# Three calls that make weight pieces further ahead around a Strassen-form down projection (hybrid encoder, one core)

## The chip, the cores and the metric

The kernel runs on one core of a Trainium2 chip. The metric is device time in microseconds (us), the median of several runs. Where a traced execution is used, its own time and span stand beside it.

## The reference

Two residual layers on 512 tokens of width 1024, each a token mixer followed by a gated MLP. Layer 0 mixes by gated linear attention, layer 1 by grouped-query softmax attention. The change touches the MLP alone, which is the same in both layers:

```python
def conv_ffn(h, w_up, w_conv, b_conv, w_down):
    u = h @ w_up
    u = lax.conv_general_dilated(
        u, w_conv[:, None, :], window_strides=(1,), padding=[(1, 1)],
        dimension_numbers=('NWC', 'WIO', 'NWC'), feature_group_count=u.shape[-1]) + b_conv
    val, gate = jnp.split(u, 2, axis=-1)
    return (jax.nn.silu(gate) * val) @ w_down
...
        x = x + conv_ffn(rmsnorm(x, norm_ffn[i]), ffn_w_up[i], ffn_w_conv[i],
                         ffn_b_conv[i], ffn_w_down[i])
```

`w_up` is 1024 x 5632 and `w_down` 2816 x 1024, all in float32.

## The kernel before

**Arithmetic.** Every float32 operand of a matmul is split in a high half (a copy to fp32r, made by ScalarE) and a low half (the rest, made by VectorE, or by a negated copy and an accumulating DMA from POOL's queue, `flush`). Each product is three matmuls, high x high, high x low, low x high (`mm3`).

**The MLP of a layer** (`ffn`, L658). The 22 tiles of 128 hidden features are walked in order, m = 0 to 21. `act_up(m)` (L664) computes two up tiles of 128 x 512 sums, t = 0 for the value into a PSUM bank of tag "acc" (three banks) and t = 1 for the gate into one of tag "s" (two banks), 24 matmuls each. What is called convolution m here follows in the trace: L683 scales the sums by the norm, L685 to L687 form the width-3 convolution, once for each t; then L689 and L690 apply the gate.

**The down projection** has two forms. Tiles 0 to 15 go pairwise into a seven-product (Strassen-like) form in two *parts* of four pairs: part 0 stands at m = 9 and part 1 at m = 17 (`DOWN_AFTER`, L45). `prepare` (L699) builds the sums of activations of a pair. `down_part` (L723) walks four *strips* of weights, n = 0 to 3, with seven products of 12 matmuls of 128 x 256 in each (L741); `begin(n)` (L745) is a strip's first product. For part 0 the pair of tiles 8 and 9 is prepared inside the part, at L777. Tiles 16 to 21 are *plain*: `split` at L796 writes their halves into a tile that L795 takes from the 22 buffers of tag "g", and they are multiplied in a last stage (L806 on).

The matmuls of `begin(0)` are traced between up tiles (m, 0) and (m, 1), at L673; the rest of the part behind convolution m, at L804.

**The weights** (class `Weights`, L111). `todo` is one list of all pieces in a fixed order. Around a part it reads: up(m, 0), strip 0 piece 0, up(m, 1), strip 0 pieces 1, 2, 3, strip 1 pieces 0 to 3, and so on. `piece(src, i, h, ahead)` (L200) flushes, makes pieces from the list until the wanted one is there, then makes more until `ahead` pieces beyond it are made, and returns it. To make a piece of an up strip is a load of 1 MB by SP's queue into one of two raw buffers (for a strip's first piece), L194 on ScalarE and L195 on VectorE. A down strip holds four blocks a21, a11, a12, a22 in one raw buffer and has four pieces, made by `summed` (L144):

- piece 0: two sums on VectorE (L151 into a new "g" tile of L149, L152 in place), then L177 and L178 for the halves
- piece 1: a third sum (L156), halves into `sh` and `sl`, of which there is one buffer each
- piece 2: two copies on ScalarE (L173, L174), the low half finished by a POOL DMA at the next flush (L184)
- piece 3: a fourth sum (L163), halves L165 and L166

The high and low halves of the other pieces have three buffers each.

**The order of work.** The source order is the order of the trace. The framework then orders each engine's queue at build time: among the instructions that its own model of time holds ready, the one that was traced first goes ahead. So an instruction that is traced late may run early, in a gap, and one that is traced early has precedence; TensorE's queue is ordered in the same way. Waits and buffer assignments are made by the framework.

Of the kernel before, what the change touches and what calls it, by code (L numbers as in the profile page):

```python
# [44 lines left out]
DOWN_AFTER = {9: 0, 17: 1}  # L45
# [9 lines left out]
def hybrid_encoder_kernel(  # L55
# [36 lines left out]
    def bank(tag, n):  # L92
        return pp.tile([P, S], F32, tag=tag, bufs=PS[tag], name=nm(n))
# [4 lines left out]
    def big(dt, n):  # L98
        return pair("g", 22, dt, n)

    def tmp(tag, n, w=S):
        return sp.tile([P, w], F32, tag=tag, bufs={"u": 4, "t": 6, "sq": 3}[tag], name=nm(n))
# [110 lines left out]
    W = Weights()  # L213
    up = [w_up[i] for i in range(2)]
# [127 lines left out]
    def feature_steps(wh, wl, hl, ps):  # L342

        for k in range(KC):
            sl = slice(k * P, (k + 1) * P)
            mm3(ps, wh[:, sl], wl[:, sl], *hl[k], k == 0, k == KC - 1)
            if k == 2:
                W.flush()
            yield

    def feature_tile(*a):
        for _ in feature_steps(*a):
            pass
# [303 lines left out]

    def ffn(layer, norm, cw, nxt):  # L658
        w_dn = down_w[layer]
        plain = {}  # L660
        down = []
        quads = {}

        def act_up(m):  # L664

            res, pss = [], []
            for t in range(2):
                ps = bank("s" if t else "acc", "up")
                feature_tile(*W.half(up[layer], 2 * m + t, 3 if m in DOWN_AFTER and t else 1), norm.hl, ps)
                pss.append(ps)  # L670
                if t == 0 and m in DOWN_AFTER:
                    down.append(down_part(DOWN_AFTER[m], m))
                    next(down[-1])  # L673
                if m == 0 and t == 0:
                    norm.tokens()
                elif m == 0:
                    norm.rows()
            for t in range(2):
                ps = pss[t]
                cc = ((layer * 2 + t) * FC + m) * 4  # L680
                w = lambda i: cw[:, cc + i : cc + i + 1]
                u = tmp("u", "u")
                dve.tensor_tensor(u, ps, norm.R, ALU.mult)  # L683
                y = tmp("t", "y")
                act.activation(y, u, AF.Identity, scale=w(1), bias=w(3))  # L685
                dve.scalar_tensor_tensor(y[:, 1:], u[:, : S - 1], w(0), y[:, 1:], ALU.mult, ALU.add)  # L686
                dve.scalar_tensor_tensor(y[:, : S - 1], u[:, 1:], w(2), y[:, : S - 1], ALU.mult, ALU.add)  # L687
                res.append(y)
            act.activation(res[1], res[1], AF.Silu)  # L689
            dve.tensor_tensor(res[0], res[0], res[1], ALU.mult)  # L690
            return res[0]
# [100 lines left out]
        for m in range(FC):  # L792
            y = act_up(m)
            if m >= 2 * NQ * NPART:
                t = big(F32R, "gu")  # L795
                split(y, t)  # L796
                plain[m] = (t[:, :S], t[:, S:])
            elif m % 2 == 0:
                last = y
            elif m not in DOWN_AFTER:  # L800
                prepare(m // 2, last, y)
            if m in DOWN_AFTER:
                late = last, y
                for _ in down[-1]:  # L804
                    pass
# [224 lines left out]
    norms = [Norm(i) for i in range(4)]  # L1030
    cw = gla(norms[0], norms[1])
    ffn(0, norms[1], cw, norms[2])
    attention(norms[2], norms[3])
    ffn(1, norms[3], cw, None)


# [86 lines left out]
```

## Time and profile before

| | us |
|---|---|
| median of three runs | 1139.58 |
| lowest and highest | 1138.07, 1140.77 |
| the profiled execution, device time | 1138.57 |
| the profiled execution, span of its instructions | 1136.4 |
| TensorE matmul busy in the span | 1119.8 |
| VectorE busy in the span | 795.5 |
| ScalarE busy in the span | 551.6 |

How to read the lines that follow in the prediction. PE is TensorE, DVE is VectorE, ACT is ScalarE, POOL is GpSimd; PEld is the load of weights into TensorE, which overlaps its matmuls. A line of the order of time has the start, the duration, the engine, the source line, the operation, output and input; in brackets stands the idle time of the engine just ahead of it and what ended it. A line of the groups has the busy time and the mean in ns of one instruction, then the idle time ahead of the group. Matmuls are pipelined, so that a matmul of 128 x 512 is listed with 0.39 us and the next one starts 0.23 us after it. A line of the table by stretches has the stretch, its length, and for each engine busy time and count. A busy matmul says nothing of its clock: the granted clock stands in a column of its own (1.00 is full).

### The profile page before, as it was taken

The page shows a single profiled execution, that of the slowest core. Times are in us where ns is not written, and L with a number is a line of the kernel's source. Part 1 is how long each engine was busy: PE and PEld are TensorE (multiplying, and loading weights), DVE is VectorE, ACT ScalarE, POOL GpSimd, SP SyncE. Part 2 cuts the span into 40 slices and gives each one's busy share as a digit, 9 for nine tenths or more (in the row PEclk, how much of TensorE's full clock was granted, in tenths as well). Part 3 has the DMA queues.
Part 4 walks back from the last instruction along what each step waited for, and adds up shares of the span by engine and source line. Part 5 has one row for each costly group of instructions (what it writes and reads, how often), then busy time and mean ns, then how long its engine had stood idle before and what let it go on. Part 6 is the DMA issues. An engine that isn't in the chain of part 4 may idle for free.

```text
span 1136.4 us, 14630 instructions
## 1 busy us (share of the span) xinstructions
PE 1119.8 (99%) x5836; PEld 960.1 (84%) x5836; DVE 795.5 (70%) x1220; ACT 551.6 (49%) x818; POOL 120.2 (11%) x114
## 2 busy tenths in 40 slices
PE   9999999999999999899999999999999999989998
PEld 7888888888889888798888888888888998879887
DVE  6787563667889577775765689766788957777572
ACT  5565233435457344463464667644445634446340
POOL 0104110001011001000004433000100100100000
PEclk9999999999999999899999999999999999999999
DMA  6422211222335332353247633223223543235321
GB/s 230 149 74 79 83 62 38 78 108 74 108 97 154 125 111 74 94 152 127 93 126 189 149 75 75 57 75 111 74 87 107 159 130 111 75 93 149 127 77 74
DMA packets 22291, 120.14 MB, mean 106 GB/s; under 512 B 2640, under 2 KB 3280, under 8 KB 10704
## 3 DMA queue, kind: packets, MB, share of 16 engines
q1 hardware_dynamic: 17328, 102.29, 26.4%
q0 software_dynamic: 4608, 16.78, 7.7%
q8 instruction: 45, 0.74, 0.3%
q14 instruction: 22, 0.18, 0.0%
q10 hardware_dynamic: 288, 0.15, 0.0%
HBM read 100.34 MB, written 2.10 MB: 90 GB/s over the span
## 4 chain that ended last, share of the span: by engine, by line
PE 92%; DVE 3%; issue 2%; DMA 1%; ACT 1%; POOL 0%; SPq 0%; DVEq 0%; POOLq 0%; ACTq 0%
PE up L338 13%; PE up L339 13%; PE up L340 13%; PE r L741 12%; PE vg L369 8%; PE op L395 8%; PE dn L339 2%; PE dn L340 2%; PE dn L338 2%; PE o L620 2%; PE pt L984 1%; DMA wl<-raw 1%; PE av L369 1%; PE kv L596 1%; PE A L338 1%
## 5 line engine op out<-in xcount | busy, mean ns | idle before, releaser
L338 PE MATMUL up<-xhl,wh 128*128 128x512 f32 x704 | 275.3, 391 | 0.0
L339 PE MATMUL up<-xhl,wh 128*128 128x512 f32 x704 | 274.7, 390 | 0.0
L340 PE MATMUL up<-xhl,wl 128*128 128x512 f32 x704 | 274.2, 390 | 0.0
L194 ACT ACTIVATE wh<-raw 128x1024 fp32r<-128x1024 f32 x132 | 139.5, 1057 | 228.0 <-PE up L339 108.2
L195 DVE TENSOR_TENSOR wl<-raw,wh 128x1024 fp32r<-128x1024 f32 x132 | 164.6, 1247 | 40.4 <-ACT wh L194 40.4
L340 PEld LDWEIGHTS up<-xhl,wl 128*128 128x128 f32 x704 | 132.4, 188 | 27.6
L338 PEld LDWEIGHTS up<-xhl,wh 128*128 128x128 f32 x704 | 132.5, 188 | 27.2
L339 PEld LDWEIGHTS up<-xhl,wh 128*128 128x128 f32 x704 | 132.6, 188 | 27.0
L741 PE MATMUL r<-gu,wh 128*128 128x256 f32 x640 | 119.6, 287 | 8.3 <-ACT wh L177 8.1
L741 PEld LDWEIGHTS r<-gu,wh 128*128 128x128 f32 x640 | 101.5, 195 | 10.0 <-ACT wh L177 9.6
L683 DVE TENSOR_TENSOR u<-up,R 128x512 f32<-128x512 f32 x88 | 60.3, 687 | 58.6 <-PE up L340 58.6
L741 PE MATMUL r<-gu,wl 128*128 128x256 f32 x320 | 91.5, 287 | 2.6 <-DMA wl<-raw 2.5
L685 ACT ACTIVATE y<-u,cw 128x512 f32<-128x512 f32 x88 | 71.2, 811 | 42.9 <-DVE u L683 42.9
L369 PE MATMUL vg<-wh,xhl 128*128 128x512 f32 x256 | 80.2, 392 | 0.5 <-DVE halfneg L256 0.5
L686 DVE SCALAR_TENSOR_TENSOR y<-u,cw,y 128x511 f32<-128x511 f32 x88 | 65.6, 747 | 8.3 <-ACT y L685 8.3
L395 PE MATMUL op<-oT,wh 128*128 128x512 f32 x256 | 70.9, 395 | 0.0
L687 DVE SCALAR_TENSOR_TENSOR y<-u,cw,y 128x511 f32<-128x511 f32 x88 | 65.8, 750 | 2.3
L689 ACT ACTIVATE y<-y 128x512 f32<-128x512 f32 x44 | 27.8, 633 | 77.6 <-DVE y L687 77.6
L741 PEld LDWEIGHTS r<-gu,wl 128*128 128x128 f32 x320 | 61.9, 194 | 3.8 <-DMA wl<-raw 3.2
L184 POOL DMA_DIRECT2D wl<-raw x32 | 28.3, 885 | 327.3 <-ACT wl L138 157.6
L369 PEld LDWEIGHTS vg<-wh,xhl 128*128 128x128 f32 x256 | 48.5, 190 | 10.7 <-ACT sq L312 0.7
L395 PEld LDWEIGHTS op<-oT,wh 128*128 128x128 f32 x256 | 47.1, 188 | 9.6 <-ACT oT L635 0.3
(220 smaller groups left out, 1990.9 us busy)
## 6 DMA issues: line engine op xcount, KB each, us to landing
raw<-in_w_up_dram SPq DMA_DIRECT2D x44, 1024.0 KB, 4.8
raw<-in_w_down_dram SPq DMA_DIRECT2D x22, 1024.0 KB, 4.8
wl<-raw POOLq DMA_DIRECT2D x32, 512.0 KB, 4.6
raw<-in_w_vg_dram SPq DMA_DIRECT2D x6, 1024.0 KB, 4.8
raw<-in_w_akq_dram SPq DMA_DIRECT2D x5, 1024.0 KB, 5.0
raw<-in_w_kq_dram SPq DMA_DIRECT2D x4, 1024.0 KB, 4.8
raw<-in_w_gout_dram SPq DMA_DIRECT2D x4, 1024.0 KB, 4.7
raw<-in_w_aout_dram SPq DMA_DIRECT2D x4, 1024.0 KB, 4.8
```

Of the source, the lines that this page charges most:

```text
L194: act.activation(hi[:, sl], r[:, sl], AF.Copy)
L195: dve.tensor_tensor(lo[:, sl], r[:, sl], hi[:, sl].bitcast(F32), ALU.subtract)
L338: mm(ps, wh, mh, start=start, stop=False)
L339: mm(ps, wh, ml, start=False, stop=False)
L340: mm(ps, wl, mh, start=False, stop=stop)
L369: mm(ps[j][:, :width], hl[k][i == 2][:, j * P : (j + 1) * P], (wl if i == 1 else wh)[:, sl], start=k == 0 and i == 0, stop=k == KC - 1 and ...
L395: mm(pss[ng][n], wt[:, sl], mv, start=k == 0 and i == 0, stop=k == KC - 1 and i == 2)
L683: dve.tensor_tensor(u, ps, norm.R, ALU.mult)
L685: act.activation(y, u, AF.Identity, scale=w(1), bias=w(3))
L686: dve.scalar_tensor_tensor(y[:, 1:], u[:, : S - 1], w(0), y[:, 1:], ALU.mult, ALU.add)
L687: dve.scalar_tensor_tensor(y[:, : S - 1], u[:, 1:], w(2), y[:, : S - 1], ALU.mult, ALU.add)
L741: mm(dst, w[:, sl], m, start=start and j == 0 and a == 0, stop=j == NQ - 1 and a == 2, skip_group_check=True)
```

## The change

```diff
     def ffn(layer, norm, cw, nxt):
         w_dn = down_w[layer]
+
+        ahead = {(m + i // 2, i % 2): n for m in DOWN_AFTER for i, n in ((-1, 2), (0, 2), (1, 5))}
         plain = {}
...
                 ps = bank("s" if t else "acc", "up")
-                feature_tile(*W.half(up[layer], 2 * m + t, 3 if m in DOWN_AFTER and t else 1), norm.hl, ps)
+                feature_tile(*W.half(up[layer], 2 * m + t, ahead.get((m, t), 1)), norm.hl, ps)
                 pss.append(ps)
```

The number of pieces made ahead was 1, and 3 at up(m, 1) for m = 9 and 17. Now it is 2 at up(m-1, 1), 2 at up(m, 0) and 5 at up(m, 1). Worked through the list of pieces, these are made at each point of the trace:

| point of the trace | before | after |
|---|---|---|
| up(m-1, 1) | up(m, 0) | up(m, 0), strip 0 piece 0 |
| convolution m-1 | | |
| up(m, 0) | strip 0 piece 0 | up(m, 1) |
| `begin(0)` | up(m, 1), strip 0 pieces 1, 2 | strip 0 pieces 1, 2 |
| up(m, 1) | strip 0 piece 3 | strip 0 piece 3, strip 1 pieces 0, 1 |
| convolution m | | |
| product with strip 0 piece 1 | strip 1 piece 0 | |
| product with strip 0 piece 2 | strip 1 piece 1 | |
| `begin(1)` and on | strip 1 piece 2, 3, ... | the same |

The order of the pieces among themselves stays, as does every instruction.

## The prediction

> **What bounds the kernel now.** I read the page first, then the table of busy time by stretch for the four parts of the down projection, then the order of time on TensorE, VectorE and ScalarE around them.
>
> ```profile
> span 1136.4 us, 14630 instructions
> ...
> PE 1119.8 (99%) x5836; PEld 960.1 (84%) x5836; DVE 795.5 (70%) x1220; ACT 551.6 (49%) x818; POOL 120.2 (11%) x114
> ...
> PEclk9999999999999999899999999999999999999999
> ...
> L741 PE MATMUL r<-gu,wh 128*128 128x256 f32 x640 | 119.6, 287 | 8.3 <-ACT wh L177 8.1
> ...
> L741 PE MATMUL r<-gu,wl 128*128 128x256 f32 x320 | 91.5, 287 | 2.6 <-DMA wl<-raw 2.5
> ```
>
> TensorE sets the end: it is idle for 1136.4 - 1119.8 = 16.6 us only, and 10.9 us of that stand ahead of L741, the products of the down parts. Only work ahead of L741 can be gained, so each part is timed from the end of the up tile (m, 0) to the first matmul of up tile (m+1, 0), m = 9 and 17 in both layers:
>
> ```profile
> core 0: us, PE busy (x) PEld busy (x) DVE busy (x) ACT busy (x) POOL busy (x), PEclk, DMA share, GB/s
> 334.17:379.76 45.59, 45.59 (x362) 44.63 (x360) 39.53 (x63) 28.05 (x41) 6.01 (x6) 1.00 0.63 178
> 461.39:516.30 54.91, 49.19 (x361) 47.12 (x361) 40.35 (x61) 30.17 (x42) 3.46 (x4) 0.94 0.53 147
> 875.22:921.00 45.78, 45.78 (x362) 44.69 (x360) 39.45 (x63) 27.70 (x41) 5.84 (x6) 1.00 0.63 177
> 1002.63:1056.42 53.79, 48.55 (x362) 46.45 (x361) 40.37 (x61) 30.07 (x42) 3.49 (x4) 0.97 0.53 151
> ```
>
> All four do the same matmuls (some 361 instructions each). The parts behind m = 9 run without idle time, at clock 1.00. Those behind m = 17 take 54.91 - 45.59 = 9.32 us and 53.79 - 45.78 = 8.01 us longer. In the order of time on TensorE:
>
> ```profile
> 461.16 0.39 PE L340 MATMUL up<-xhl,wl 128*128 128x512 f32 x1
> 465.59 1.22 PE L741 MATMUL r<-gu,wh 128*128 128x256 f32 x4 [4.04 <-ACT wh L177]
> ...
> 491.61 0.39 PE L741 MATMUL r<-gu,wl 128*128 128x256 f32 x1 [1.55 <-DMA wl<-raw]
> ...
> 1006.83 1.21 PE L741 MATMUL r<-gu,wh 128*128 128x256 f32 x4 [4.04 <-ACT wh L177]
> ...
> 1031.34 0.39 PE L741 MATMUL r<-gu,wl 128*128 128x256 f32 x1 [0.94 <-DMA wl<-raw]
> ```
>
> and by stretches, with the granted clock as the third column from the right:
>
> ```profile
> 461.40:465.60 4.20, 0.16 (x2) 0.01 (x1) 3.79 (x7) 2.03 (x4) 0.00 (x0) 0.83 0.00 0
> 465.60:471.00 5.40, 5.40 (x20) 4.90 (x21) 4.07 (x5) 4.79 (x7) 0.88 (x1) 0.50 0.41 123
> 471.00:516.30 45.30, 43.63 (x342) 42.21 (x341) 32.49 (x51) 23.33 (x34) 2.58 (x3) 1.00 0.59 164
> ```
>
> So the 9.32 us of layer 0 have three terms. **4.20** us of waiting (461.39 to 465.59). Then the granted clock is 0.50 from 465.6 to 471: half of 5.4, about **2.7** us, is lost in matmuls that the page counts as busy. The rest, 9.32 - 4.20 - 2.7 = **2.4** us, lies behind 471, with 1.55 us of it ahead of the matmul at 491.61 (its low half comes by DMA). The 4.20 us can't be had without the 2.7 us.
>
> **Why m = 17 waits and m = 9 doesn't.** VectorE and ScalarE at m = 9, layer 0:
>
> ```profile
> 327.61 0.68 DVE L683 TENSOR_TENSOR u<-up,R 128x512 f32<-128x512 f32 x1
> 328.21 0.68 DVE L151 TENSOR_TENSOR sum<-raw 128x512 f32<-128x512 f32 x1
> ...
> 329.70 1.06 ACT L177 ACTIVATE wh<-raw 128x1024 fp32r<-128x1024 f32 x1 [0.55 <-DVE raw L152]
> ...
> 333.19 1.22 DVE L195 TENSOR_TENSOR wl<-raw,wh 128x1024 fp32r<-128x1024 f32 x1
> ...
> 335.60 0.40 PE L338 MATMUL up<-xhl,wh 128*128 128x512 f32 x1
> ...
> 337.99 0.69 DVE L690 TENSOR_TENSOR y<-y,y 128x512 f32<-128x512 f32 x1
> ...
> 339.19 0.69 DVE L151 TENSOR_TENSOR sum<-raw 128x512 f32<-128x512 f32 x1
> ```
>
> and at m = 17:
>
> ```profile
> 454.83 0.69 DVE L683 TENSOR_TENSOR u<-up,R 128x512 f32<-128x512 f32 x1
> ...
> 456.40 0.75 DVE L686 SCALAR_TENSOR_TENSOR y<-u,cw,y 128x511 f32<-128x511 f32 x1 [0.89 <-ACT y L685]
> ...
> 461.72 0.69 DVE L690 TENSOR_TENSOR y<-y,y 128x512 f32<-128x512 f32 x1 [0.76 <-ACT y L689]
> 462.32 0.69 DVE L151 TENSOR_TENSOR sum<-raw 128x512 f32<-128x512 f32 x1
> 462.44 0.63 ACT L696 ACTIVATE gu<-y 128x512 fp32r<-128x512 f32 x1 [0.76 <-DVE y L690]
> ...
> 464.48 1.06 ACT L177 ACTIVATE wh<-raw 128x1024 fp32r<-128x1024 f32 x1 [1.41 <-DVE raw L152]
> ...
> 480.11 0.63 ACT L696 ACTIVATE gu<-y 128x512 fp32r<-128x512 f32 x1 [0.76 <-DVE y L690]
> ...
> 480.33 0.69 DVE L151 TENSOR_TENSOR sum<-raw 128x512 f32<-128x512 f32 x1
> ```
>
> At m = 9 the first sum of strip 0 (L151) slips in behind the first L683 of convolution 8, though it is traced behind that whole convolution. At m = 17 it doesn't: VectorE idles 0.89 us at 456.40 rather than start it, and L151 follows at once when L690 of convolution 16 is over. The difference in the code: tile 16 is the first plain one (its number is not below 16), so its `split` takes a tile of tag "g" at L795, ahead in the trace of the "g" tile that L149 takes for the sums. Both times L151 starts within 0.22 us of an L696 that first writes such a tile (462.32 beside 462.44, 480.33 behind 480.11). I read this as: tiles of one tag are handed out in traced order, so a sum traced behind a plain convolution waits for that convolution's end. It is a reading; the trace shows the coincidence, not the cause.
>
> **The change part by part.** No instruction is added or removed and no DMA: the queue of pieces keeps its order, and each `make` issues what it did. Three points of the trace move.
>
> (1) Piece 0 of strip 0 is made at up(m-1, 1), ahead of convolution m-1, instead of at up(m, 0). Its "g" tile then precedes that of tile 16; the last ones ahead of it are those of `prepare` 7, traced before tile 16. So at m = 17 L151 may take the place of L683 at 454.83, as VectorE is free there. By the rows above, L151 at 328.21 was followed by L177 at 329.70, 1.49 us later: L177 would start at 454.83 + 1.49 = 456.3, end at 457.4, and the low half (L178, 1.22 us like the L195 row) by about 459 to 460. TensorE wants it at 461.39. The wait of 4.20 us goes, and with it the 2.7 us at half clock. What pays is convolution 16: L683 comes 2 x 0.69 = 1.4 us later or, with the 1.22 us of L178 as well, 2.6 us. Tile 16 itself is first used in the plain stage at the end of the layer; the PSUM bank that L683 frees is wanted by the second sum bank of the part, behind 461.39, so some 4 us of cover remain. Cost taken: 0; without the cover, up to 2.6 us a part.
>
> (2) Piece up(m, 1) is made at up(m, 0) and no longer inside `begin(0)`. On ScalarE and VectorE nothing stands between the two points in the trace; only matmuls do. Cost 0. What is late next is just this piece: its L195 ended at 333.19 + 1.22 = 334.41 for an up tile that began at 335.60, 1.19 us of slack at m = 9. At m = 17, L690 and the L697 of a plain tile (0.69 us each) have precedence over it. Bounds for a new wait: 0 (as at m = 9), and 2 x 0.69 + 1.4 - 1.19 = 1.6 us a part. I take 0, the row of the same code nearest to it, and keep 1.6 for the range.
>
> (3) Pieces 0 and 1 of strip 1 are made at up(m, 1), ahead of convolution m, instead of inside the products. At m = 17 that puts strip 1's "g" tile ahead of tile 17's, so its L151 no longer waits for 480.33. Its raw strip can only be loaded when the L195 of up(m, 1) is done with the buffer, which also comes earlier now. At m = 9 the same L151 ran at 339.19, 339.19 - 334.17 = 5.0 us into the part, against 480.33 - 461.39 = 18.9 us at m = 17. Strip 1 thus moves some 14 us forward, and its third piece, strip 2's sums and the DMAs on POOL's queue behind them move with it. This takes the 2.4 us of layer 0 and the matching part of layer 1's 8.01 us. `sh` has one buffer: piece 1 of strip 1 still can't be written until strip 0's products are through, as before. At m = 9 all this ran greedily already, without a wait; cost 0, and at most the 1.19 us of slack spent.
>
> **Sum.** 9.32 + 8.01 = 17.3 us. The profiled execution took 1138.57 us for its span of 1136.4 (2.2 us lie around it): 1138.57 - 17.3 = 1121.2. The median of the three runs, 1139.58, is 1.0 us above the profiled one; against it the result is 1122.3. I predict **1122.3**.
>
> A wait that is cut but not removed has its price from rows of two kinds: 1.55 us left the clock at 1.00, 4.04 us brought it to 0.50, and nothing lies between, so a remainder of 3 us is bounded by 3.0 and 3.0 + 2.7 us. [...]
>
> **The rivals.**
>
> *Half of it.* The wait at 461.39 goes, but (2) leaves 1.6 us ahead of up(17, 1), and strip 1 or 2 still waits for a low half by DMA (1.55 and 0.94 us now). For: VectorE is busy 39.5 of 45.6 us even in the good parts, and the low halves come by the same queue. Against: the good parts have that same load and no wait. Time: 1122.3 + 2 x 1.6 + 1.55 + 0.94 = 1128.0.
>
> *The change doesn't do what it says.* If L151 waits at m = 17 for something else that ends with convolution 16, moving it in the trace does nothing there, and m = 9 had nothing to gain: 1139.6, the time before. For: the cause is only inferred. Against: any reason that rests on traced order is lifted too.
>
> *Slower: the second up piece falls behind a whole convolution.* Place: L195 of up(m, 1), in all four parts. It is now traced right behind convolution m-1, with the sums ahead of both; if convolution m-1 were taken to its end first, L195 would follow L690, at 337.99 + 0.69 = 338.7 at m = 9, and end at 339.9, 4.3 us past 335.60. That is a wait as long as the one seen, so 4.3 + 2.7 = 7.0 us. In the two parts at m = 9 it is new, 14.0 us; at m = 17 it replaces the present wait of 4.20 + 2.7, and only the ends are gained (2.4, and 8.01 - 6.9 = 1.1 us): 1139.6 + 14.0 - 3.5 = 1150.1. It decides from the point where L195 ends 1.19 us later than at present, and it outweighs the gain only with the clock lost. For: 1.19 us is little. Against: L195 was behind the same convolution before, and ran at 333.19, well ahead of its L690 at 337.99.
>
> **How the numbers follow.** Forecast 0.68, half of it 0.16, no effect 0.07, slower 0.09. What this kernel's runs can tell from no change is about 0.2%, 2.3 us: the first two are faster (0.84), the third the same (0.07), the last slower (0.09). The range holds the first two. Its low end is the fastest run less the sum and about 1 us of spread, 1138.07 - 17.3 - 1.3 = 1119.5; its high end is half of it, 1128.0, and 1 us: 1129.
>
> **What would show it.** Right: both stretches from the end of up(17, 0) to up(18, 0) near 45.7 us; no wait for `wh` of L177 ahead of L741; clock 1.00 throughout, and the PEclk digit 8 in the seventeenth slice a 9; L151 of strip 0 at m = 17 ahead of or among convolution 16, L151 of strip 1 about 5 us into the part; the page's idle time ahead of L741 near nothing; the parts at m = 9 still near 45.6. Wrong: L151 still directly behind L690 of convolution 16 (the second rival), TensorE waiting for L195 ahead of up(9, 1) or up(17, 1) (the third, or half of it), or DMA waits of over 1 us behind the first strip.

## The result and the profile after

| | before | after |
|---|---|---|
| median, us | 1138.84 (1138.07 to 1140.77, 4 runs) | 1120.49 (1119.98 to 1120.88, 4 runs) |
| ratio | | 0.9836, 95% interval 0.9819 to 0.9853 |
| profiled execution, us | 1138.57, span 1136.4 | 1119.98, span 1117.8 |

The change is 18.35 us faster. The forecast was 1122.3 us. The median before is now taken over four runs; the prediction had three. Source lines behind L660 have moved by two: the products are now L743, the convolution L685 to L692, the plain split L698 and L699.

The page after, the parts that answer to those of before (the counts of each engine's work are the same):

```profile
span 1117.8 us, 14636 instructions
...
PE 1112.3 (100%) x5836; PEld 955.5 (85%) x5836; DVE 793.9 (71%) x1220; ACT 551.5 (49%) x818; POOL 120.4 (11%) x114
...
PEclk9999999999999999999999999999999999999999
```

and two of its groups, kept apart by shape:

```profile
L743 PE MATMUL r<-gu,wh 128*128 128x256 f32 x640 | 116.4, 282 | 0.0
...
L743 PE MATMUL r<-gu,wl 128*128 128x256 f32 x320 | 90.4, 283 | 0.0
```

TensorE's idle time fell from 16.6 to 5.5 us, and the idle time ahead of the products from 10.9 us to nothing. The mean of a product with a high half went from 287 to 282 ns: the granted clock is 1.00 in all four parts, where it was 0.94 and 0.97 in those at m = 17 before. The four parts, each from the end of up(m, 0) to the first matmul of up(m+1, 0):

```profile
333.30:378.89 45.59, 45.59 (x362) 44.62 (x360) 39.52 (x62) 28.04 (x41) 6.03 (x6) 1.00 0.62 177
460.52:506.11 45.59, 45.59 (x362) 44.63 (x360) 37.22 (x58) 27.46 (x39) 3.47 (x4) 1.00 0.62 177
865.02:910.61 45.59, 45.59 (x362) 44.63 (x360) 39.53 (x62) 28.03 (x41) 5.86 (x6) 1.00 0.62 177
992.24:1037.83 45.59, 45.59 (x362) 44.63 (x360) 37.22 (x58) 27.45 (x39) 3.49 (x4) 1.00 0.63 178
```

All four take the same 45.59 us at full clock. Against before that is 9.32 + 8.20 us at m = 17 and 0.19 us at m = 9 of layer 1, 17.71 us in all. The rest of the 18.6 us between the two spans is the start: part 0 of layer 0 begins at 333.30, against 334.17 before, 0.87 us sooner, in work that the change doesn't touch. A second traced execution of the same changed kernel, told of below as e7, begins that part at 333.97.

VectorE at m = 17 of layer 0, after:

```profile
453.96 0.68 DVE L151 TENSOR_TENSOR sum<-raw 128x512 f32<-128x512 f32 x1
454.56 0.68 DVE L685 TENSOR_TENSOR u<-up,R 128x512 f32<-128x512 f32 x1
...
457.62 1.22 DVE L178 TENSOR_TENSOR wl<-raw,wh 128x1024 fp32r<-128x1024 f32 x1
...
460.08 1.22 DVE L195 TENSOR_TENSOR wl<-raw,wh 128x1024 fp32r<-128x1024 f32 x1
...
463.61 0.69 DVE L692 TENSOR_TENSOR y<-y,y 128x512 f32<-128x512 f32 x1
...
466.21 0.68 DVE L151 TENSOR_TENSOR sum<-raw 128x512 f32<-128x512 f32 x1
```

The first sum of strip 0 starts at 453.96 instead of 462.32, ahead of the L685 of convolution 16, and the low half it leads to is done at 457.62 + 1.22 = 458.84, 1.7 us before TensorE reaches it at 460.52. Strip 1's sum starts 466.21 - 460.52 = 5.7 us into the part instead of 18.9.

### The profile page after: what moved, and what is told of

Same layout as the page of the kernel before. It is cut to its first block, busy times and chain, and to the rows that moved or that the text cites. A ratio compares the mean times of both kernels' runs of the same rounds, so it can differ in the third digit from the quotient of the medians.

```text
span 1117.8 us, 14636 instructions
## 1 busy us (share of the span) xinstructions
PE 1112.3 (100%) x5836; PEld 955.5 (85%) x5836; DVE 793.9 (71%) x1220; ACT 551.5 (49%) x818; POOL 120.4 (11%) x114
## 4 chain that ended last, share of the span: by engine, by line
PE 99%; DVE 0%; DMA 0%; ACT 0%; issue 0%; SPq 0%; DVEq 0%; ACTq 0%
PE r L743 14%; PE up L338 14%; PE up L339 14%; PE up L340 14%; PE vg L369 8%; PE op L395 8%; PE dn L338 2%; PE dn L340 2%; PE dn L339 2%; PE o L620 2%; PE pt L986 1%; PE av L369 1%; PE kv L596 1%; PE A L338 1%; PE A L340 1%; PE A L339 1%
## 5 line engine op out<-in xcount | busy, mean ns | idle before, releaser
L195 DVE TENSOR_TENSOR wl<-raw,wh 128x1024 fp32r<-128x1024 f32 x132 | 164.5, 1246 | 40.0 <-ACT wh L194 40.0
L743 PE MATMUL r<-gu,wh 128*128 128x256 f32 x640 | 116.4, 282 | 0.0
L743 PEld LDWEIGHTS r<-gu,wh 128*128 128x128 f32 x640 | 99.7, 191 | 0.3
L685 DVE TENSOR_TENSOR u<-up,R 128x512 f32<-128x512 f32 x88 | 60.3, 687 | 54.3 <-PE up L340 54.3
L743 PE MATMUL r<-gu,wl 128*128 128x256 f32 x320 | 90.4, 283 | 0.0
L687 ACT ACTIVATE y<-u,cw 128x512 f32<-128x512 f32 x88 | 71.2, 811 | 32.9 <-DVE u L685 32.7
L743 PEld LDWEIGHTS r<-gu,wl 128*128 128x128 f32 x320 | 61.1, 191 | 0.0
```

Of the source, the lines that this page charges most:

```text
L195: dve.tensor_tensor(lo[:, sl], r[:, sl], hi[:, sl].bitcast(F32), ALU.subtract)
L743: mm(dst, w[:, sl], m, start=start and j == 0 and a == 0, stop=j == NQ - 1 and a == 2, skip_group_check=True)
```

## The experiments

In what follows "part excess" is the length of a part, measured as above, less 45.59 us. Each ratio is against the kernel before, run on the same chip.

**e1: step (1) alone.**

```diff
-                feature_tile(*W.half(up[layer], 2 * m + t, 3 if m in DOWN_AFTER and t else 1), norm.hl, ps)
+                feature_tile(*W.half(up[layer], 2 * m + t, 3 if m in DOWN_AFTER and t else 2 if t and m + 1 in DOWN_AFTER else 1), norm.hl, ps)
```

> Only step (1): piece 0 of strip 0 is made at up(m-1, 1); the rest as before. Theory: the wait of 4.20 us and the 2.7 us at half clock go in both layers, 13.8 us; strip 1's sums still start behind convolution 17, so the 3.5 us behind the first strip stay or grow, by up to some 2 us a layer, since TensorE now reaches strip 1 sooner: 1125 to 1129 us. If the first wait hung on step (2) or (3): 1138.8 us, no change.

1124.33 us, ratio 0.9875 (0.9858 to 0.9893). The expectation was 1125 to 1129 us, so the time lies 0.7 us below it. One of the four runs took 1128.70 us, at a mean granted clock of 0.998 where the others had 0.999 or 1.000; it wasn't traced, and its cause is open. The order of time on TensorE has only these waits left at m = 17 (the first two in layer 0):

```profile
475.74 0.51 PE L741 MATMUL r<-gu,wh 128*128 128x256 f32 x2 [0.17 <-ACT wh L177]
483.79 0.38 PE L741 MATMUL r<-gu,wl 128*128 128x256 f32 x1 [1.36 <-DMA wl<-raw]
...
1009.57 0.51 PE L741 MATMUL r<-gu,wh 128*128 128x256 f32 x2 [0.17 <-ACT wh L177]
...
1017.18 0.39 PE L741 MATMUL r<-gu,wl 128*128 128x256 f32 x1 [0.92 <-DMA wl<-raw]
```

The wait of 4.04 us and the half clock are gone by this step alone (the granted clock is 1.00 in both parts at m = 17). The part excess is 47.74 - 45.59 = 2.15 us in layer 0 and 47.31 - 45.59 = 1.72 us in layer 1: what lay behind the first strip did not grow, which the expectation had allowed for. Strip 1's sum is still held by convolution 17:

```profile
471.76 0.69 DVE L690 TENSOR_TENSOR y<-y,y 128x512 f32<-128x512 f32 x1 [0.17 <-ACT y L689]
...
472.70 0.69 DVE L151 TENSOR_TENSOR sum<-raw 128x512 f32<-128x512 f32 x1
```

**e2: step (2) alone.**

```diff
-... 3 if m in DOWN_AFTER and t else 1), norm.hl, ps)
+... (3 if t else 2) if m in DOWN_AFTER else 1), norm.hl, ps)
```

> Only step (2): piece up(m, 1) is made at up(m, 0). Theory: nothing of the work changes place by more than a matmul; 1138.8 us, within 0.2%. If the late second up piece were part of the wait: up to some 1 to 3 us a layer faster.

1138.97 us, ratio 0.9996 (0.9987 to 1.0005): no change, as expected.

**e3: step (3) alone.**

```diff
-... 3 if m in DOWN_AFTER and t else 1), norm.hl, ps)
+... 5 if m in DOWN_AFTER and t else 1), norm.hl, ps)
```

> Only step (3): pieces 0 and 1 of strip 1 are made at up(m, 1). Theory: the first wait and the lost clock stay, the 2.4 + 1.1 us behind the first strip go: 1135.3 us. If the DMA waits there come from something else than strip 1's late sums: 1138.8 us.

1133.76 us, ratio 0.9953 (0.9941 to 0.9966). The first wait is as before (4.05 and 4.04 us), and the DMA waits at m = 17 are gone. The part excess there is 6.04 us in layer 0 and 5.75 us in layer 1, against 9.32 and 8.20: some 2.4 us less in layer 1, where the half clock lasted 3.41 us as before, and 3.3 us in layer 0, where it lasted 3.41 us in place of 6.83 (more on this below).

**e4: all three steps, at m = 17 alone.**

```diff
-        ahead = {(m + i // 2, i % 2): n for m in DOWN_AFTER for i, n in ((-1, 2), (0, 2), (1, 5))}
+        ahead = {(m + i // 2, i % 2): n for m in (17,) for i, n in ((-1, 2), (0, 2), (1, 5))}
...
-... ahead.get((m, t), 1)), norm.hl, ps)
+... ahead.get((m, t), 3 if m in DOWN_AFTER and t else 1)), norm.hl, ps)
```

> All three steps at m = 17 alone; at m = 9 as before. Theory: the gain is all at m = 17, and m = 9 was unhindered: 1120.5 us, the same as the change as given within 0.2%, and 45.6 us for the parts at m = 9. If steps at m = 9 gained or lost anything: off 1120.5 us by over 2 us.

1121.90 us, ratio 0.9848 (0.9833 to 0.9863), against 0.9836 (0.9819 to 0.9853) for the whole change: the intervals overlap. The traced execution has 45.58 or 45.59 us in each of the four parts, so that as far as the parts show it, the gain is all at m = 17. The 1.4 us between the medians isn't explained by them.

**e5: nothing moved in the trace, a tag of its own for the sums.** This is the test of the cause that the prediction could only infer.

```diff
-                sums["e"] = e = big(F32, "sum")
+                sums["e"] = e = pair("sum", 2, F32, "sum")
...
-        return pair("g", 22, dt, n)
+        return pair("g", 20, dt, n)
```

> The kernel before, with nothing moved in the trace; only the tile of the sums gets a tag of its own (two buffers; tag g has 20 in place of 22). Theory (tiles of one tag are handed out in traced order, and the plain tile stands ahead of the sums): the sums are free of convolutions 16 and 17, both waits at m = 17 go, 1120.5 to 1123 us. Rival (a sum goes behind the convolution because it is traced behind it): 1138.8 us.

1122.20 us, ratio 0.9847 (0.9832 to 0.9862). Built with 20 buffers in "g" and the sums left there, the kernel has every engine's queue in the order of before, so the smaller tag is not what acts. Nor do buffers run short: when the first sum at m = 17 is handed its tile, 16 of the 22 are in use (14 with the operands of part 1, one with tile 16, one with the sum itself). VectorE of e5, layer 0:

```profile
448.54 0.69 DVE L151 TENSOR_TENSOR sum<-raw 128x512 f32<-128x512 f32 x1
...
451.01 0.69 DVE L690 TENSOR_TENSOR y<-y,y 128x512 f32<-128x512 f32 x1
...
467.55 0.68 DVE L151 TENSOR_TENSOR sum<-raw 128x512 f32<-128x512 f32 x1
```

The L690 at 451.01 is that of convolution 15: the sum of strip 0 runs ahead of it, although it is traced behind convolution 16. Both parts at m = 17 take 45.59 us. Those at m = 9 take 46.44 and 46.43 us, with new waits of 0.58 and 0.57 us on TensorE for L750 (ScalarE's copy of a product's sums), so e5 stays 1.7 us behind the change.

**Three kernels that put the wait back in steps.** They start from e5 and hold the first sum behind a chosen instruction of convolution 16 in VectorE's queue (`W.last` is what `summed` queues L151 and L152 behind). For the second L687:

```diff
+                held = dve.scalar_tensor_tensor(y[:, : S - 1], u[:, 1:], w(2), y[:, : S - 1], ALU.mult, ALU.add)
+                if m == 16 and t:
+                    W.last = held
```

and in the same way for L690 and for the second L686.

> As the kernel with a tag of its own for the sums, but the first two sums of the strips made next are queued behind L690 of convolution 16, where they stood before the change. Theory: strip 0 waits 4.2 us and loses 2.7 us at half clock in each layer, strip 1 stays early: 1120.5 + 13.8 = 1134.3 us. Rival (the wait was of the tag's buffers, not of the place in the queue): 1120.5 to 1123 us.

> The same, queued behind the second L687 of convolution 16: the sums start about 1.45 us sooner than behind L690, so TensorE waits 4.20 - 1.45 = some 2.75 us in each layer. If the clock stays at 1.00 for a wait of that length: 1120.5 + 5.5 = 1126.0 us. If it falls as it did at 4.04 us: 1120.5 + 2 x (2.75 + 2.7) = 1131.4 us.

> The same, queued behind the second L686 of convolution 16, some 2.2 us sooner than behind L690: a wait of some 2.0 us in each layer. Clock kept: 1120.5 + 4.0 = 1124.5 us. Clock lost: 1120.5 + 2 x (2.0 + 2.7) = 1129.9 us.

| held behind | median, us | ratio, 95% interval | waits at the first products, both layers | part excess |
|---|---|---|---|---|
| L690 | 1134.13 | 0.9952 (0.9937 to 0.9967) | 3.37 | 5.64, 6.20 |
| second L687 | 1132.73 | 0.9933 (0.9915 to 0.9952) | 1.93 + 0.52 | 4.35, 2.97 |
| second L686 | 1126.82 | 0.9888 (0.9872 to 0.9905) | 1.67 or 1.68 | 2.41, 2.41 |
| nothing (e5) | 1122.20 | 0.9847 (0.9832 to 0.9862) | none | 0, 0 |

Only the place of the first sum in VectorE's queue is set differently in these four, and each earlier place gives less waiting and a shorter time. Held at L690 a wait for L177 is back, of 3.37 us and not of the 4.04 us of before. That 1134.13 us meets the 1134.3 us expected is partly luck: the two parts cost 5.64 + 6.20 = 11.84 us in place of 13.8, and the 1.7 us that e5 loses at m = 9, which all three kernels have too, were left out. The same 1.7 us are missing from the other two expectations; with them, 1124.5 us for the second L686 with the clock kept becomes 1126.2, beside 1126.82 measured at clock 1.00.

The kernel held behind the second L687 expected either a kept or a lost clock. It shows both in one execution. The same waits in layer 0 and in layer 1, on TensorE:

```profile
463.95 0.74 PE L743 MATMUL r<-gu,wh 128*128 128x256 f32 x4 [1.93 <-ACT wh L177]
465.21 0.58 PE L743 MATMUL r<-gu,wl 128*128 128x256 f32 x1 [0.52 <-DVE wl L178]
...
1000.83 0.74 PE L743 MATMUL r<-gu,wh 128*128 128x256 f32 x4 [1.93 <-ACT wh L177]
1002.09 0.39 PE L743 MATMUL r<-gu,wl 128*128 128x256 f32 x1 [0.52 <-DVE wl L178]
```

and by stretches, the granted clock being the third column from the right:

```profile
465.00:468.20 3.20, 2.99 (x12) 2.90 (x13) 3.20 (x5) 3.20 (x5) 0.00 (x0) 0.50 0.18 23
...
1001.40:1005.40 4.00, 3.48 (x22) 2.96 (x21) 4.00 (x5) 3.97 (x5) 0.00 (x1) 1.00 0.16 25
```

The clock fell to 0.50 in layer 0 and stayed at 1.00 in layer 1. The four runs are 1129.57 us (this one) and 1132.71 to 1133.02 us. The others had a mean granted clock of 0.996 where the traced one had 0.998, so they lost more of it; in which layer isn't on record, since they weren't traced.

**e6: steps (1) and (3) without (2)**, and **e7: the change once more beside it.**

```diff
-... 3 if m in DOWN_AFTER and t else 1), norm.hl, ps)
+... 5 if m in DOWN_AFTER and t else 2 if t and m + 1 in DOWN_AFTER else 1), norm.hl, ps)
```

> Steps (1) and (3) without (2). Theory: step (2) costs and brings nothing, so this is the change as given: 1120.5 us within 0.2%, all four parts at 45.6 us. If the earlier second up piece is what keeps TensorE from waiting ahead of up(17, 1) once the first wait is gone: a wait of 1 to 3 us a layer there, 1122.5 to 1126.5 us.

> The change as given, beside it on the same chip. 1120.5 us, within 0.2%; the stretch ahead of the first part, which is built alike in all kernels, may again differ by up to 1 us from run to run.

1120.52 us, ratio 0.9836 (0.9820 to 0.9852), beside 1120.43 us, ratio 0.9834 (0.9819 to 0.9849). All parts of both take 45.59 us. Step (2) is worth nothing, with or without the others.

No version beat the change: TensorE is busy for 1112.3 of 1117.8 us, and no wait is left in the parts.

## Why the prediction was right, step by step

**The bound and the place.** The forecast came from one comparison inside the profile of before: the same matmuls took 45.59 us where nothing waited and up to 54.91 us where something did. It gave 17.3 us; the parts gave 17.71. The 0.4 us between lies in layer 1, where 45.78 us was taken for the floor and 45.59 is it. The rest, up to the 18.35 us between the medians, is within its interval of 16.7 to 20.6 us (0.0147 and 0.0181 of 1138.84). Of the 1.8 us by which the forecast of 1122.3 us was too high, 0.7 us come from the median before, which is 1138.84 with the fourth run.

**The cause.** Inferred before from L151 following an L696 twice, now shown as far as kernels can: e5 takes only the shared tag away and both waits go; e1 lets strip 0's sum pass the plain tile and leaves strip 1's behind the next one, and just that one still waits. The rival "the change doesn't do what it says" falls. No run shows the framework's handing out of tiles itself; the cause is shown by what moves when the tag changes.

**Step (1)** was right: L151 at 453.96, low half at 458.84, where 459 to 460 was forecast. What pays is convolution 16, as forecast: its last instruction, L692, starts 463.61 - 460.52 = 3.1 us into the part, where the L690 of before started 461.72 - 461.39 = 0.3 us into it. It had the cover it was given, since no matmul of the part waits.

**Step (2)** was costed at nothing and is (e2, e6). Its L195 was named as next to be late, behind the gate of convolution 16. It ran ahead of that gate (L692) and ended at 460.08 + 1.22 = 461.30 for an up tile that began at 461.95:

```profile
461.95 0.40 PE L338 MATMUL up<-xhl,wh 128*128 128x512 f32 x1
```

So 0.65 us of slack is left where m = 9 had 1.19 before. The third rival needed that slack to be gone: it was 0.65 us short of a first wait, and further from the 4.3 us that it was priced at.

**Step (3)** was right in kind: e3 alone removes the DMA waits at m = 17, and e1, without it, keeps them (1.36 and 0.92 us). The forecast that strip 1 would start about 5 us into the part held (5.7).

**The terms that were mis-sized.** The split of layer 1 was wrong: it took 2.7 us for the lost clock there too and so left 1.1 us for the strips. In the trace of before the half clock lasted 6.83 us in layer 0 and 3.41 us in layer 1. These stretches are cut just inside it:

```profile
464.35:470.95 6.60, 5.36 (x19) 4.89 (x20) 5.32 (x7) 5.86 (x8) 0.88 (x1) 0.50 0.32 96
...
1006.90:1010.20 3.30, 3.30 (x13) 3.08 (x14) 3.30 (x3) 3.30 (x4) 0.00 (x0) 0.50 0.10 15
```

The second cost half of 3.41, some 1.7 us, and the strips 8.20 - 4.20 - 1.7 = 2.3 us, about as much as the 2.4 us of layer 0. The sum wasn't touched, because it was made from whole parts and not from these pieces. The expectation of 1135.3 us for e3 rested on the 1.1 us and came out 1.5 us too high.

**The price of a wait that is cut but not removed.** The prediction's bounds for a remainder of 3 us were 3.0 and 5.7 us. A wait with the clock lost and one with the clock kept both occur, even below 3 us: 1.93 + 0.52 us of waiting cost 4.35 us in layer 0, where the clock fell to 0.50, and 2.97 us in layer 1, where it stayed at 1.00.

## What to carry to other kernels

Where a scheduler hands out the buffers of a tag in traced order, as this one behaves, a tile that is late to be written can hold up the later tiles of its tag while buffers are free; an idle engine beside a ready instruction is the sign, and a tag of its own, or an earlier place in the trace, is the cure. Two stages of one kernel that do the same work are the best price list for each other: the whole difference in their length is safer than a sum of the waits that one can name. A wait of the busiest engine can cost more than its length: here some 2.7 us were lost at a clock of 0.50 behind a wait of 4.04 us, by the estimate made from the trace of before, and the busy share doesn't show that part.

## What the runs showed of the hardware that was not expected

The time at half clock behind a wait came in two lengths in the seven cases that were read in rows of 0.5 us, where a clock between 1.00 and 0.50 gives the point of a change. It lasted 3.41 us where the clock fell between 0.3 us ahead of the end of the first wait and 1.0 us behind it (layer 1 of before, both layers of e3, layer 0 of the kernels held at L687 and L690), and 6.83 us where it fell 1.3 or 1.4 us ahead of it (layer 0 of before, layer 1 of the kernel held at L690). The two of the kernel held at L690, cut just inside the half clock:

```profile
466.30:469.55 3.25, 3.25 (x13) 3.06 (x14) 3.25 (x5) 2.71 (x3) 0.24 (x1) 0.50 0.24 45
1002.35:1008.95 6.60, 5.52 (x20) 5.03 (x21) 6.01 (x8) 6.00 (x8) 0.87 (x1) 0.50 0.31 98
```

So the same wait of 3.37 us lost some 1.7 us at half clock in one layer (half of 3.41) and some 2.8 us in the other (half of the 5.5 us from its end, 1003.43, to the clock's return).

Not every wait brought the clock down. It fell at all six of 4.0 to 4.1 us (two each of before, e2 and e3; e2's parts had a mean clock of 0.94 and 0.97, as in before) and at both of 3.37 us. With 1.93 + 0.52 us of waiting it fell in layer 0 of the kernel held at L687, at 464.90, and not in layer 1. It stayed at 1.00 with the 1.67 and 1.68 us of the kernel held at L686 and with the 1.36 and 0.92 us of e1. What decides between a fall and none, or between the two lengths, no run shows.

At m = 9 of layer 1 the load of strip 1 landed at different times in kernels that load the same strip there. VectorE's wait for it was 1.04 us in before, 3.08 us in e2 and 2.54 us in e3; e2's part took 47.81 us and e3's 47.72 us, where before had 45.78. The row of e2:

```profile
882.50 0.69 DVE L151 TENSOR_TENSOR sum<-raw 128x512 f32<-128x512 f32 x1 [3.08 <-DMA raw<-in_w_down_dram]
```

In layer 0 the same strip came without a wait of VectorE in before and in e2. The edits of e2 and e3 also move points of the trace at m = 9; whether that or the load itself made the difference was not tried.
